# Activations at one place per quarter in 16-byte steps, low weights of the second ring 16 bytes further at each use, and a changed order of the rings

## The chip, the cores and the metric

The kernel runs on one core of a Trainium2 chip. Its time is the device time in microseconds; the median of three runs before the change is 2704.8 us (2704.26 to 2705.38). The core has five engines with queues of their own: TensorE (PE in the profile, its weight loads PEld), VectorE (DVE), ScalarE (ACT), GpSimd (POOL) and SyncE (SP), which issues most of the loads. All of them work on one on-chip memory of 128 partitions; "address" below means the byte within a partition.

## The reference

One inference step of a two-layer decoder on 256 prompt positions and 8 x 8 sample positions, 2048 features. Layer 0 mixes tokens with gated linear attention, layer 1 with a causal spatial gate; each is followed by an MLP with a squared ReLU, and each sublayer by a layer norm over the scaled residual.

```python
def sq_relu_mlp(x, w1, w2):
    return jnp.square(jax.nn.relu(x @ w1)) @ w2
...
            if i % N_MIXERS == 0:
                h, s = gla_mixer(x, gla_w_in[j], gla_w_gate[j], gla_b_gate[j], gla_norm_g[j],
                                 gla_w_out[j], gla_state0[j])
...
            else:
                h, v_rows = sg_mixer(x, sg_w_in[j], sg_b_in[j], sg_v_norm_g[j], sg_v_norm_b[j],
                                     sg_w_spatial[j], sg_b_spatial[j], sg_w_out[j])
...
            x = layer_norm(DEEPNORM_ALPHA * x + h, ln1_g[i], ln1_b[i])
            x = layer_norm(DEEPNORM_ALPHA * x + sq_relu_mlp(x, mlp_w1[i], mlp_w2[i]), ln2_g[i], ln2_b[i])
```

The arithmetic is float32; the kernel keeps it by splitting every factor into a high and a low part and adding three products.

## The kernel before

**Layout and tiles.** Prompt and sample positions stand side by side as 320 columns (`T`); the 2048 features are 16 feature tiles (`KT`) of 128 partitions. A large product `out = W^T x` is cut into column blocks of 256 output features (`UN`), which are two tiles of 128 in PSUM, and into four quarters of the input features (`NU`), four feature tiles each (`UK`). One column block of one quarter is a *unit*: a weight block of 4 x 256 columns, 512 KB in HBM.

**A unit** (`unit`, L129) loads the block into `raw` (SP's queue, three buffers), copies it to the high part `wh` on ACT (L144) and subtracts to get the low part `wl` on DVE (L145). `group` (L165) runs over the quarters and over the column blocks given, and issues for each unit 2 x 4 times the three matmuls of `mm3` (L158): low weights by high activations (L161), high weights by low activations (L162), high weights by high activations (L163). So a unit is 24 matmuls. While a matmul runs, the weights of the next one are loaded into the array.

**Rings.** `wh` and `wl` have buffers in two rings, "a" and, from layer 0's output product on, "b"; each has four buffers of each part. `next_ring` (L154) takes the rings in turn, a b a b, so quarter q of a group of one column block always finds the same ring.

**Activations.** Pairs of buffers hold a high and a low part for all 16 feature tiles: pair "a" (`a0`, `a1`) and pair "b" (`b0`, `b1`). `yh`, `yl` are the normed inputs of an MLP or of the spatial gate, `hh`, `hl` the MLP's hidden activations for 2048 of its 8192 hidden features at a time; `xh`, `xl`, `oh`, `ol` belong to layer 0's mixer; `dgh`, `dgl` are the centred activations times the norm's gain, which the first two column blocks after a norm read while the norm's own values are still being made (322 columns, the last two carry corrections).

**Where things stand.** The kernel places buffers by hand with small filler tiles. `bigtile` (L198) starts the 320 columns of a feature tile 128 bytes into the buffer (`LINE // 2` numbers of 4 bytes), and each further feature tile 1280 bytes on, which is 5 x 256. With the fillers, every activation of `x`, `o`, `y` and `h` begins at 128 past a multiple of 256, every `wh` at 0 and every `wl` at 64 (`Ring.part` puts a gap of 64 bytes before the first `wl`). `dg` starts at 0 and its feature tiles lie 1288 bytes apart, so each begins 8 bytes further than the one before. The weights of the small gate projection (`wgp`, L316 and L317) begin at 224.

**Order.** The order of instructions is made by the tile framework's scheduler from the order in which the code issues them; within an engine they then run in that order. In an MLP (`mlp`, L843) the four quarters c of the hidden features follow each other: `w1` by `y` (eight column blocks), then `w2` by `h` (eight column blocks), added into `z`. In the spatial gate `y` is read for v (L933), for u (L990) and, overwritten by the gated product, for the output (L993).

Of the kernel before, what the change touches and what calls it, by code (L numbers as in the profile page):

```python
# [9 lines left out]
F32R = mybir.dt.float32r  # L10
# [5 lines left out]
P = 128  # L16
D = 2048
KT = D // P
TP = 256
DB, DS = 8, 8  # L20
T = TP + DB * DS
# [9 lines left out]
UK = 4  # L31
UN = 256
NU = KT // UK
WARM = 9
LINE = 64
BIG = KT * T + LINE


V_BG, V_NG = 0, 8
V_L1G, V_L1B, V_L2G, V_L2B = 24, 56, 88, 120  # L40
V_SB, V_SG, V_SBB = 152, 184, 200
# [3 lines left out]
class Ring:  # L45


    def __init__(self, pool, tag):
        self.pool, self.tag, self.gap = pool, tag, False

    def part(self, p, name):

        t = self.pool.tile([P, UK, UN], F32R, tag=p + self.tag, name=name)
        if not self.gap:
            self.pool.tile([P, LINE // 4], F32, tag="gap", name=name + "_gap", bufs=1)
            self.gap = True
        return t


class Side:  # L60
# [17 lines left out]
def step_kernel(ctx: ExitStack, tc: tile.TileContext, A):  # L78
# [3 lines left out]
    def nm(s):  # L82
        uid[0] += 1
        return f"{s}_{uid[0]}"
# [11 lines left out]
    rings = [Ring(wa, "a")]  # L96
# [4 lines left out]
    def mmtile(n=T):  # L101

        if mx is not None:
            banks[0] = (banks[0] + 1) % 6
        return (mx if banks[0] > 3 else mm).tile([P, n], F32, tag="mm", name=nm("mm"), padded_shape=[P, 512])
# [19 lines left out]
    def col(c):  # L125
        return vec[:, c : c + 1]


    def unit(w, row0, q, col0, ring):  # L129

        raw = wraw.tile([P, UK, UN], F32, tag="raw", name=nm("raw"))
        src = w[row0 // (UK * P) + q, col0 // UN]
        hi = ring.part("h", nm("wh"))
        lo = ring.part("l", nm("wl"))
        units[0] += 1
        step = 2 if units[0] <= 2 else UK
        for k in range(0, UK, step):
            nc.sync.dma_start(raw[:, k : k + step, :], src[:, k : k + step, :])
        step = 1 if units[0] == 1 else step
        for k in range(0, UK, step):  # L140
            ks = slice(k, k + step)
            if units[0] == 1:
                before_unit(k)
            nc.scalar.copy(hi[:, ks, :], raw[:, ks, :])  # L144
            nc.vector.tensor_sub(lo[:, ks, :], raw[:, ks, :], hi[:, ks, :].bitcast(F32))  # L145
        return hi, lo
# [7 lines left out]
    def next_ring():  # L154
        turn[0] += 1
        return rings[turn[0] % len(rings)]
# [7 lines left out]

    def group(w, row0, cols, rh, rl, evict, side=None, width=T, before=None):  # L165

        ps = [mmtile(width) for _ in range(2 * len(cols))]
        for q in range(NU):
            if before is not None:
                before(q)  # L170
            for i, c in enumerate(cols):
                wh, wl = unit(w, row0, q, c, next_ring())
                for n in range(2):
                    for kk in range(UK):
                        k = q * UK + kk
                        mm3(ps[2 * i + n][:], wh, wl, kk, n, rh, rl, k, 0, width, k == 0, k == KT - 1)
                if side is not None:
                    side()
        for n in range(2 * len(cols)):
            evict(n, ps[n])  # L180
# [14 lines left out]
    w_in = A["gla_w_in"]  # L195
    C_Q, C_K, C_V, C_R = 0, H * DK, 2 * H * DK, 2 * H * DK + H * DV

    def bigtile(tag, dt, name, width=T):  # L198

        t = (lp if tag == "b1" else big).tile([P, BIG], dt, tag=tag, name=nm(name))
        start = LINE // 2 if width == T else 0
        return t[:, start : start + KT * width].rearrange("p (k t) -> p k t", t=width)

    def parts(pair, name, width=T):
        return bigtile(pair + "0", F32R, name + "h", width), bigtile(pair + "1", F32R, name + "l", width)

    xh, xl = parts("a", "x")  # L210
    o_all = bigtile("b0", F32, "o_all")

# [26 lines left out]
    def before_unit(k):  # L239

        x_parts(slice(k, k + 1), first_x[k // 2][:, k % 2 : k % 2 + 1, 0:T])
# [89 lines left out]
    class Head:  # L331


        def __init__(hd, h):
            hd.h = h
            hd.eb, hd.ei, hd.ee = {}, {}, {}
# [331 lines left out]
    def second_half():  # L668

        nonlocal lp, l2, z, gl, mx  # L670
        side.flush()
        split_o(range(4 * (H - 1), 4 * H))
        gst.close()
        gls.close()
        gl = ctx.enter_context(tc.tile_pool(name="gs", bufs=2, space=bass.MemoryType.PSUM))
        mx = ctx.enter_context(tc.tile_pool(name="mx", bufs=2, space=bass.MemoryType.PSUM))
        banks[0] = 3
        lp = ctx.enter_context(tc.tile_pool(name="lp", bufs=1))
        l2 = ctx.enter_context(tc.tile_pool(name="l2", bufs=2))
        wb = ctx.enter_context(tc.tile_pool(name="wb", bufs=4))  # L680
        rings.append(Ring(wb, "b"))
        wb.tile([P, LINE // 4], F32, tag="fill", name="fill_b", bufs=1)
        z = lp.tile([P, KT, T], F32, tag="z", name="z")
        lp.tile([P, 3 * LINE // 4], F32, tag="fill", name="fill_l")
        for q in range(2):
            nc.gpsimd.dma_start(z[:, 8 * q : 8 * q + 8, :], xT[:, 8 * q : 8 * q + 8, :])
# [120 lines left out]
                  lambda n, ps, i=i: evict(2 * i + n, ps), side, before=before if i == 0 else before_last if i == D // UN - 1 else None)  # L807
            i += n2

    def gemm_of(norm, out, w, col0, evict_raw, evict):  # L810

        yh, yl = parts(out, "y")
        norm.close()
        side = Side([lambda j=j: norm.apply(j, yh, yl) for j in range(KT)], 3 * NU)
        group(w, 0, (col0, col0 + UN), *norm.raw, evict_raw, side, width=TW)
        side.flush()
        for i in range(2, D // UN):
            group(w, 0, (col0 + i * UN,), yh, yl, lambda n, ps, i=i: evict(2 * i + n, ps))
        return yh, yl
# [23 lines left out]
    def mlp(i, norm, y_in, h_in, vg, vb, raw, last=False):  # L843

        w1, w2 = A["mlp_w1"][i], A["mlp_w2"][i]
        NC_ = 4
        for c in range(NC_):
            hs = []

            def sq_relu(j, x, r):  # L850
                if not hs:
                    hs.extend(parts(h_in, "h"))
                hh, hl = hs
                f = l2.tile([P, T], F32, tag="f", name=nm("f"))
                nc.vector.scalar_tensor_tensor(f[:], x, 0.0, r[:], op0=ALU.max, op1=ALU.mult)
                nc.scalar.copy(hh[:, j, 0:T], f[:])  # L856
                nc.vector.tensor_sub(hl[:, j, 0:T], f[:], hh[:, j, 0:T].bitcast(F32))  # L857

            def evict(j, ps):
                r = l2.tile([P, T], F32, tag="r", name=nm("r"))  # L860
                nc.scalar.activation(r[:], ps[:], AF.Relu)
                sq_relu(j, ps[:], r)

            def evict_raw(j, ps):
                t, wb_ = norm.correct(ps)
                r = l2.tile([P, T], F32, tag="r", name=nm("r"))
                nc.scalar.activation(r[:], t[:], AF.Relu, bias=wb_)
                sq_relu(j, r[:], r)

            if c == 0:  # L870
                yh, yl = gemm_of(norm, y_in, w1, 0, evict_raw, evict)
            else:
                gemm(w1, 0, c * D, yh, yl, evict)
            if c < NC_ - 1:
                def evz(j, ps, s=ALPHA if c == 0 else 1.0):
                    nc.vector.scalar_tensor_tensor(z[:, j, :], z[:, j, :], s, ps[:], op0=ALU.mult, op1=ALU.add)
                gemm(w2, c * D, 0, *hs, evz)
            else:
                return residual_gemm(w2, *hs, c * D, 1.0, vg, vb, raw, last=last)


    def before(q):
        if q == NU - 1:
            second_half()
        else:
            split_o(range(UK * q, UK * (q + 1)))

    norm = residual_gemm(A["gla_w_out"], oh, ol, 0, ALPHA, V_L1G, V_L1B, "b", quad=True,
                         side=side, before=before)
    norm = mlp(0, norm, "a", "b", V_L2G, V_L2B, "a")  # L890


# [21 lines left out]
    def put_v(j, x, bias):  # L914
        nonlocal v, nv
        if j == 0:
            v = bigtile("a0", F32, "v")
            nv = Norm(v, V_SG, V_SBB)
        vj = v[:, j, 0:T]
        nc.scalar.activation(vj, x, AF.Gelu, bias=bias)  # L920
        if j >= KT // 2:
            nc.vector.tensor_sub(vj, vj, nv.c[:])
        nv.add(j)
        if j == 3:
            spatial()
# [4 lines left out]
        nc.vector.tensor_add(bias[:], wb_, col(V_SB + KT + j))  # L930
        put_v(j, t[:], bias[:])

    yh, yl = gemm_of(norm, "b", A["sg_w_in"], D, ev_v_raw, lambda j, ps: put_v(j, ps[:], col(V_SB + KT + j)))  # L933

    nv.close()
    oV = A["o_vT"].rearrange("(k p) t -> p k t", p=P)
# [55 lines left out]

    norm = residual_gemm(A["sg_w_out"], ph, pl, 0, ALPHA, V_L1G + KT, V_L1B + KT, "a", quad=True)  # L993
    norm = mlp(1, norm, "b", "a", V_L2G + KT, V_L2B + KT, "b", last=True)


# [4 lines left out]
    ps = {}  # L1001
# [23 lines left out]
    for j in range(KT):  # L1025
        y, g, b = z[:, j, :], col(norm.vg + j), col(norm.vb + j)
# [4 lines left out]
        else:  # L1031
            if j not in ps:
                put_d(j)
            t = l2.tile([P, T], F32, tag="t", name=nm("t"), bufs=3)
# [70 lines left out]
```

## Time and profile before

| | before |
|---|---|
| median of 3 runs | 2704.8 us |
| the profiled execution | 2703.75 us |
| its span, first to last instruction | 2702.0 us |
| granted TensorE clock over the span | 0.999 |
| read from HBM, written | 409.60 MB, 22.02 MB |
| matmuls with `yh`, `yl` | 7872 |
| matmuls with `hh`, `hl` | 6144 |
| matmuls with `xh`, `xl`, `oh`, `ol`, of the three lines | 3072 |
| matmuls with `dgh`, `dgl`, of the three lines | 576 |

How to read the lines quoted below: a group of instructions is "line engine operation out<-in shapes xcount | busy us, mean ns of one | idle us of the engine just before them". A row of the timeline is "start us, duration us, engine line operation". A row of windows is "stretch: its length, busy time of the engine (count) clock, DMA share, GB/s". Matmuls overlap their neighbours, so the duration of one is about twice the distance between two starts.

### The profile page before, as it was taken

How to read it: one execution, taken by the hardware profiler on the slowest of the kernel's cores; microseconds unless marked ns; L12 is line 12 of the kernel's file. 1: busy time of each engine (PE TensorE's matmuls, PEld its weight loads, DVE VectorE, ACT ScalarE, POOL GpSimd, SP SyncE). 2: the span in 40 equal slices, each digit the busy share in tenths (PEclk: the TensorE clock that was granted, in tenths of full speed). 3: DMA queues.
4: the chain of work that ended last, by engine and by line, in shares of the span. 5: the costliest groups of instructions: out<-in, count | busy, mean ns of one | idle time of the engine just before them, and what ended most of it. 6: DMA issues, size and time to landing. Idle time of an engine off the chain costs nothing.

```text
span 2702.0 us, 44679 instructions
## 1 busy us (share of the span) xinstructions
PE 2692.4 (100%) x18515; PEld 2669.7 (99%) x18515; DVE 1543.5 (57%) x2289; ACT 1182.8 (44%) x1702; POOL 53.5 (2%) x83
## 2 busy tenths in 40 slices
PE   9999999999999999999999999999999999999998
PEld 9999999999999999999999999999999999999998
DVE  6667577885444444444468775587444444444456
ACT  6545455464234334333445554355334323333434
POOL 1000001000000000000001000000000000000000
PEclk9999999999999999999999999999999999999999
DMA  7656556644445455444445444454444545554442
GB/s 243 193 188 228 185 190 218 211 146 156 152 151 154 151 154 151 153 151 153 150 148 171 150 140 136 140 162 155 150 155 150 154 151 153 152 153 152 153 152 79
DMA packets 126396, 434.53 MB, mean 161 GB/s; under 512 B 13680, under 2 KB 17904, under 8 KB 126192
## 3 DMA queue, kind: packets, MB, share of 16 engines
q1 hardware_dynamic: 119136, 407.82, 48.6%
q0 software_dynamic: 6512, 23.20, 2.6%
q8 instruction: 145, 2.38, 0.4%
q10 hardware_dynamic: 544, 0.66, 0.1%
q14 instruction: 59, 0.48, 0.1%
HBM read 409.60 MB, written 22.02 MB: 160 GB/s over the span
## 4 chain that ended last, share of the span: by engine, by line
PE 99%; ACT 0%; DMA 0%; DVE 0%; issue 0%; ACTq 0%; DVEq 0%
PE mm L161 32%; PE mm L163 31%; PE mm L162 31%; PE gl L600 1%; PE gl L603 1%; PE gl L558 1%; PE gl L948 0%; PE gl L542 0%; DMA raw<-gla_w_in 0%; ACT z L1038 0%; PE gl L943 0%; DMA xr<-xT 0%; PE gl L543 0%; PE gl L458 0%; PE gl L456 0%; PE gl L521 0%
## 5 line engine op out<-in xcount | busy, mean ns | idle before, releaser
L145 DVE TENSOR_TENSOR wl<-raw,wh 128x1024 fp32r<-128x1024 f32 (+1 forms) x740 | 901.6, 1219 | 938.8 <-ACT wh L144 936.3
L144 ACT CAST wh<-raw 128x1024 fp32r<-128x1024 f32 (+1 forms) x740 | 771.3, 1044 | 1201.3 <-PE mm L163 1080.9
L163 PE MATMUL mm<-yh,wh 128*128 128x320 f32 x2624 | 805.0, 307 | 0.0
L161 PE MATMUL mm<-yh,wl 128*128 128x320 f32 x2624 | 803.1, 308 | 0.0
L162 PE MATMUL mm<-yl,wh 128*128 128x320 f32 x2624 | 794.2, 303 | 0.0
L161 PE MATMUL mm<-hh,wl 128*128 128x320 f32 x2048 | 630.8, 308 | 0.0
L163 PE MATMUL mm<-hh,wh 128*128 128x320 f32 x2048 | 628.7, 307 | 0.0
L162 PE MATMUL mm<-hl,wh 128*128 128x320 f32 x2048 | 619.6, 303 | 0.0
L162 PEld LDWEIGHTS mm<-yl,wh 128*128 128x128 f32 x2624 | 492.5, 188 | 0.0
L161 PEld LDWEIGHTS mm<-yh,wl 128*128 128x128 f32 x2624 | 490.9, 188 | 0.0
L163 PEld LDWEIGHTS mm<-yh,wh 128*128 128x128 f32 x2624 | 490.8, 187 | 0.0
L162 PEld LDWEIGHTS mm<-hl,wh 128*128 128x128 f32 x2048 | 384.4, 188 | 0.0
L161 PEld LDWEIGHTS mm<-hh,wl 128*128 128x128 f32 x2048 | 384.4, 188 | 0.0
L163 PEld LDWEIGHTS mm<-hh,wh 128*128 128x128 f32 x2048 | 383.0, 187 | 0.0
L161 PE MATMUL mm<-xh,wl 128*128 128x320 f32 x768 | 241.1, 314 | 0.9 <-DVE wl L145 0.5
L163 PE MATMUL mm<-xh,wh 128*128 128x320 f32 x768 | 236.7, 308 | 0.0
L162 PE MATMUL mm<-xl,wh 128*128 128x320 f32 x768 | 234.7, 306 | 0.0
L161 PEld LDWEIGHTS mm<-xh,wl 128*128 128x128 f32 x768 | 144.1, 188 | 5.4 <-issue 1.9
L162 PEld LDWEIGHTS mm<-xl,wh 128*128 128x128 f32 x768 | 144.3, 188 | 3.5 <-issue 1.2
L163 PEld LDWEIGHTS mm<-xh,wh 128*128 128x128 f32 x768 | 143.9, 187 | 1.3
L857 DVE TENSOR_TENSOR hl<-f,hh 128x320 fp32r<-128x320 f32 x128 | 62.3, 489 | 29.4 <-ACT hh L856 29.4
L161 PE MATMUL mm<-oh,wl 128*128 128x320 f32 x256 | 78.1, 309 | 0.6 <-DVE nw L187 0.6
(268 smaller groups left out, 2112.2 us busy)
## 6 DMA issues: line engine op xcount, KB each, us to landing
raw<-mlp_w SPq DMA_DIRECT2D x512, 512.0 KB, 3.5
raw<-gla_w_in SPq DMA_DIRECT2D x94, 512.0 KB, 4.2
raw<-sg_w_in SPq DMA_DIRECT2D x64, 512.0 KB, 3.5
st<-state SPq DMA_DIRECT2D x32, 512.0 KB, 4.3
o_state_s<-st POOLq DMA_DIRECT2D x32, 512.0 KB, 3.8
raw<-gla_w_out SPq DMA_DIRECT2D x32, 512.0 KB, 4.2
raw<-sg_w_out SPq DMA_DIRECT2D x32, 512.0 KB, 3.5
z<-xT POOLq DMA_DIRECT2D x2, 1280.0 KB, 11.6
```

The source lines that it names most:

```text
L144: nc.scalar.copy(hi[:, ks, :], raw[:, ks, :])
L145: nc.vector.tensor_sub(lo[:, ks, :], raw[:, ks, :], hi[:, ks, :].bitcast(F32))
L161: nc.tensor.matmul(ps, wl[:, kk, s], x_h, start=first, stop=False)
L162: nc.tensor.matmul(ps, wh[:, kk, s], x_l, start=False, stop=False)
L163: nc.tensor.matmul(ps, wh[:, kk, s], x_h, start=False, stop=last)
L558: nc.tensor.matmul(pu[:], hd.ktp[:, blk, kt * P : (kt + 1) * P], hd.vtp[:, blk, :], start=(blk == 0), stop=(blk == 1))
L600: nc.tensor.matmul(po[:], qm[:, kt, b * P : (b + 1) * P], part[:], start=False, stop=(b == DB - 1 and kt == 1 and part is sth))
L603: nc.tensor.matmul(pu[:], kz[:, g, i, kt * P : (kt + 1) * P], hd.vts[:, g, :], start=True, stop=True)
L857: nc.vector.tensor_sub(hl[:, j, 0:T], f[:], hh[:, j, 0:T].bitcast(F32))
```

## The change

Three things are changed for the products whose activations are `y` or `h`.

1. *Place of the activations.* A buffer of `y` or `h` is wrapped in `Rows`, which starts the four feature tiles of quarter q at `16 * places[q]` bytes past a multiple of 256 instead of 128. The MLP of layer 0 has `y` at 0, 4, 8, 12 (in 16-byte steps, quarters 0 to 3), that of layer 1 at 2, 6, 10, 14; `h` has 1, 5, 9, 13 for even c and 3, 7, 11, 15 for odd c. High and low part have the same places, but for the spatial gate, where they have 0, 2, 6, 9 and 4, 6, 8, 12.
2. *Place of the low weights in ring "b".* Its `wl` buffers are 256 bytes longer, and each use for a `Rows` product starts 16 bytes (spatial gate: 32) further than the use before in the same quarter, from 0 to 240 and round again. Each buffer of `y` or `h` has its own count, with `c0` as its start. For other products they stay at 64. Ring "a" and all `wh` keep their places.
3. *Order of the rings.* `group` takes one turn of `next_ring` more at its start for a `Rows` product, so that the units of one column block (a pair of feature tiles of the output) use the rings as a b a b and those of the next as b a b a.

```diff
+EVEN = ((0, 4, 8, 12), (2, 6, 10, 14))
+ODD = ((1, 5, 9, 13), (3, 7, 11, 15))
...
-    def __init__(self, pool, tag):
-        self.pool, self.tag, self.gap = pool, tag, False
-
-    def part(self, p, name):
-
+    def __init__(self, pool, tag, loose=False):
+        self.pool, self.tag, self.gap, self.loose = pool, tag, loose, loose
+
+    def part(self, p, name, at=None):
+
+        if p == "l" and self.loose:
+            t = self.pool.tile([P, UK * UN + LINE], F32R, tag=p + self.tag, name=name)
+            return t[:, at : at + UK * UN].rearrange("p (k n) -> p k n", n=UN)
         t = self.pool.tile([P, UK, UN], F32R, tag=p + self.tag, name=name)
...
+class Rows:
...
+    def __init__(self, buf, places, c0, cs):
+        self.buf, self.places, self.cs = buf, places, cs
+        self.c = [c0] * NU
+
+    def __getitem__(self, key):
+        p, k, t = key
+        at = 4 * self.places[k // UK] + k * T
+        return self.buf[p, at + t.start : at + t.stop]
+
+    def low(self, q):
+        c = self.c[q]
+        self.c[q] += self.cs
+        return 4 * (c % 16)
...
-    def unit(w, row0, q, col0, ring):
+    def unit(w, row0, q, col0, ring, at=LINE // 4):
...
-        lo = ring.part("l", nm("wl"))
+        lo = ring.part("l", nm("wl"), at)
...
+        if isinstance(rh, Rows):
+            next_ring()
         ps = [mmtile(width) for _ in range(2 * len(cols))]
...
-                wh, wl = unit(w, row0, q, c, next_ring())
+                ring = next_ring()
+                wh, wl = unit(w, row0, q, c, ring, rh.low(q) if ring.loose and isinstance(rh, Rows) else LINE // 4)
...
-    def bigtile(tag, dt, name, width=T):
+    def bigtile(tag, dt, name, width=T, places=None, c0=0, cs=1):
...
+        if places is not None:
+            return Rows(t, places, c0, cs)
...
-        rings.append(Ring(wb, "b"))
+        rings.append(Ring(wb, "b", True))
...
-                    hs.extend(parts(h_in, "h"))
+                    hs.extend(parts(h_in, "h", places=(ODD[c % 2], ODD[c % 2]), c0=4 * (2 * i + c // 2)))
...
-                yh, yl = gemm_of(norm, y_in, w1, 0, evict_raw, evict)
+                yh, yl = gemm_of(norm, y_in, w1, 0, evict_raw, evict, (EVEN[i], EVEN[i]))
...
-    yh, yl = gemm_of(norm, "b", A["sg_w_in"], D, ev_v_raw, lambda j, ps: put_v(j, ps[:], col(V_SB + KT + j)))
+    yh, yl = gemm_of(norm, "b", A["sg_w_in"], D, ev_v_raw, lambda j, ps: put_v(j, ps[:], col(V_SB + KT + j)),
+                     ((0, 2, 6, 9), (4, 6, 8, 12)), 2)
```

Every engine issues the same instructions as before; addresses are no part of the rows below. The scheduler moves a few rows at the start of the three stages that follow a `dg` stage. On DVE, at the end of the first `w1` product of layer 0's MLP, the casts of weights (`wl<-raw,wh`) stand among the last steps of the norm (`yl`) and the first of the hidden activations (`hl`); line numbers are 28 to 34 higher in the changed file. Before:

```order
L784 TENSOR_TENSOR t_6429<-nd_6037,z 128x320
L857 TENSOR_TENSOR hl_6373<-f_6396,hh_6372 128x320
L145 TENSOR_TENSOR wl_6797<-raw_6795,wh_6796 128x1024
L790 TENSOR_TENSOR yl_6035<-z,yh_6034 128x320
L785 SCALAR_TENSOR_TENSOR t_6423<-t_6423,vec,rstd_6038 128x320
L857 TENSOR_TENSOR hl_6373<-f_6407,hh_6372 128x320
L785 SCALAR_TENSOR_TENSOR t_6429<-t_6429,vec,rstd_6038 128x320
L145 TENSOR_TENSOR wl_6901<-raw_6899,wh_6900 128x1024
```

After:

```order
L818 TENSOR_TENSOR t_6428<-nd_6036,z 128x320
L891 TENSOR_TENSOR hl_6372<-f_6395,hh_6371 128x320
L824 TENSOR_TENSOR yl_6034<-z,yh_6033 128x320
L819 SCALAR_TENSOR_TENSOR t_6422<-t_6422,vec,rstd_6037 128x320
L891 TENSOR_TENSOR hl_6372<-f_6406,hh_6371 128x320
L819 SCALAR_TENSOR_TENSOR t_6428<-t_6428,vec,rstd_6037 128x320
L173 TENSOR_TENSOR wl_6870<-raw_6868,wh_6869 128x1024
L173 TENSOR_TENSOR wl_6840<-raw_6838,wh_6839 128x1024
```

One subtraction of weights moves from the third row to behind the norm's and the hidden activations' steps. On TensorE the same place shows the last feature tiles of `y` being used as they come, in three column blocks in turn (`mm_6436`, `mm_6569`, `mm_6570` before; numbers one lower after). Before:

```order
L162 MATMUL mm_6436<-yl_6035,wh_6528 128x320
L163 MATMUL mm_6436<-yh_6034,wh_6528 128x320
L161 MATMUL mm_6436<-yh_6034,wl_6529 128x320
L162 MATMUL mm_6569<-yl_6035,wh_6662 128x320
L163 MATMUL mm_6569<-yh_6034,wh_6662 128x320
L161 MATMUL mm_6569<-yh_6034,wl_6663 128x320
L162 MATMUL mm_6570<-yl_6035,wh_6662 128x320
L163 MATMUL mm_6570<-yh_6034,wh_6662 128x320
L161 MATMUL mm_6570<-yh_6034,wl_6663 128x320
```

After:

```order
L190 MATMUL mm_6435<-yl_6034,wh_6527 128x320
L191 MATMUL mm_6435<-yh_6033,wh_6527 128x320
L189 MATMUL mm_6435<-yh_6033,wl_6528 128x320
L190 MATMUL mm_6568<-yl_6034,wh_6661 128x320
L191 MATMUL mm_6568<-yh_6033,wh_6661 128x320
L189 MATMUL mm_6568<-yh_6033,wl_6662 128x320
L190 MATMUL mm_6434<-yl_6034,wh_6527 128x320
L191 MATMUL mm_6434<-yh_6033,wh_6527 128x320
```

The third column tile's matmuls (`mm_6569` after) come a few rows later, behind the next feature tile's for `mm_6434`. Everywhere else on TensorE the sequence of the three lines is as before.

More of the change, by code (lines that the diff above doesn't have):

```diff
@@ L196, in step_kernel, with parts @@
     C_Q, C_K, C_V, C_R = 0, H * DK, 2 * H * DK, 2 * H * DK + H * DV
-    def bigtile(tag, dt, name, width=T):
+    def bigtile(tag, dt, name, width=T, places=None, c0=0, cs=1):
         t = (lp if tag == "b1" else big).tile([P, BIG], dt, tag=tag, name=nm(name))
+        if places is not None:
+            return Rows(t, places, c0, cs)
         start = LINE // 2 if width == T else 0
         return t[:, start : start + KT * width].rearrange("p (k t) -> p k t", t=width)
-    def parts(pair, name, width=T):
-        return bigtile(pair + "0", F32R, name + "h", width), bigtile(pair + "1", F32R, name + "l", width)
+    def parts(pair, name, width=T, places=(None, None), c0=0, cs=1):
+        return (bigtile(pair + "0", F32R, name + "h", width, places[0], c0, cs),
+                bigtile(pair + "1", F32R, name + "l", width, places[1], c0, cs))
     xh, xl = parts("a", "x")
@@ L808, in gemm, with gemm_of @@
             i += n2
-    def gemm_of(norm, out, w, col0, evict_raw, evict):
-        yh, yl = parts(out, "y")
+    def gemm_of(norm, out, w, col0, evict_raw, evict, places, cs=1):
+        yh, yl = parts(out, "y", places=places, cs=cs)
         norm.close()
```

## The prediction

> **What bounds the kernel now.** I read the page's busy times and its chain first, to see which engine sets the end.
>
> ```profile
> PE 2692.4 (100%) x18515; PEld 2669.7 (99%) x18515; DVE 1543.5 (57%) x2289; ACT 1182.8 (44%) x1702; POOL 53.5 (2%) x83
> PE 99%; ACT 0%; DMA 0%; DVE 0%; issue 0%; ACTq 0%; DVEq 0%
> ```
>
> TensorE is busy for 2692.4 of 2702.0 us, and the chain that ended last lies on it for 99%. So a matmul that takes its place for a nanosecond longer moves the end by a nanosecond, and work on ACT, DVE or the queues counts only where it makes TensorE wait. The groups of instructions say which matmuls the change can reach: those whose activations are `yh`, `yl`, `hh`, `hl`.
>
> ```profile
> L163 PE MATMUL mm<-yh,wh 128*128 128x320 f32 x2624 | 805.0, 307 | 0.0
> L161 PE MATMUL mm<-yh,wl 128*128 128x320 f32 x2624 | 803.1, 308 | 0.0
> L162 PE MATMUL mm<-yl,wh 128*128 128x320 f32 x2624 | 794.2, 303 | 0.0
> L161 PE MATMUL mm<-hh,wl 128*128 128x320 f32 x2048 | 630.8, 308 | 0.0
> L163 PE MATMUL mm<-hh,wh 128*128 128x320 f32 x2048 | 628.7, 307 | 0.0
> L162 PE MATMUL mm<-hl,wh 128*128 128x320 f32 x2048 | 619.6, 303 | 0.0
> ```
>
> That is 3 x (2624 + 2048) = 14016 of the 18515 matmuls, in 584 units of 24, and none of them waited (last column 0.0). The 303 to 308 ns are lifetimes of pipelined matmuls that overlap; what counts is the distance from one start to the next. I take it from the timeline of TensorE inside a steady stage, and from a window that holds just one MLP half (256 groups of three).
>
> ```profile
> 1300.23 0.31 PE L161 MATMUL mm<-yh,wl 128*128 128x320 f32 x1
> 1300.38 0.30 PE L162 MATMUL mm<-yl,wh 128*128 128x320 f32 x1
> 1300.52 0.31 PE L163 MATMUL mm<-yh,wh 128*128 128x320 f32 x1
> 1300.66 0.31 PE L161 MATMUL mm<-yh,wl 128*128 128x320 f32 x1
> ```
>
> ```profile
> 667.13:778.06 110.93, 110.93 (x770) 1.00 0.49 152
> L161 PE MATMUL mm<-hh,wl 128*128 128x320 f32 x256 | 78.8, 308 | 0.0
> L163 PE MATMUL mm<-hh,wh 128*128 128x320 f32 x256 | 78.6, 307 | 0.0
> L162 PE MATMUL mm<-hl,wh 128*128 128x320 f32 x256 | 77.4, 303 | 0.0
> ```
>
> 110.93 us over 768 matmuls is 144.44 ns each, at a granted clock of 1.00. All of these read activations that begin 128 bytes past a multiple of 256, high weights at 0 and low weights at 64 past one. This is one fixed arrangement (worked out from the tiles' sizes and fills), kept through nearly the whole kernel.
>
> **What another arrangement costs.** The trace of before holds two other arrangements. The first is the pair of column blocks that reads the uncorrected activations `dg`: their rows have 322 columns, so each feature tile begins 8 bytes further than the one before.
>
> ```profile
> 1443.81:1472.77 28.96, 28.96 (x198) 1.00 0.48 146
> L161 PE MATMUL mm<-dgh,wl 128*128 128x322 f32 x64 | 19.9, 310 | 0.0
> L163 PE MATMUL mm<-dgh,wh 128*128 128x322 f32 x64 | 19.9, 310 | 0.0
> L162 PE MATMUL mm<-dgl,wh 128*128 128x322 f32 x64 | 19.8, 309 | 0.0
> L722 PE MATMUL gl<-lo,ones_r 128*128 128x320 f32 x2 | 0.6, 310 | 0.0
> L723 PE MATMUL gl<-hi,ones_r 128*128 128x320 f32 x2 | 0.6, 308 | 0.0
> ```
>
> 28.96 us over 196 matmuls is 147.76 ns each. Two more columns cost at most 2 x 144.44/320 = 0.9 ns of that, so some **2.4 ns** remain for the arrangement. Inside that stage the slots are uneven, as the timeline shows for its third feature tile, against 0.43 us for the three in the steady stage:
>
> ```profile
> 1444.69 0.31 PE L161 MATMUL mm<-dgh,wl 128*128 128x322 f32 x1
> 1444.83 0.31 PE L162 MATMUL mm<-dgl,wh 128*128 128x322 f32 x1
> 1444.98 0.31 PE L163 MATMUL mm<-dgh,wh 128*128 128x322 f32 x1
> 1445.14 0.31 PE L161 MATMUL mm<-dgh,wl 128*128 128x322 f32 x1
> ```
>
> Here three take 0.45 us, 150 ns each: less 0.9 for the columns that is 4.7 ns over the steady slot, the dearest end I can read. The second arrangement is the gate projection: activations at 128 as elsewhere, weights 224 bytes past a multiple of 256.
>
> ```profile
> L317 PE MATMUL gl<-xh,wgp 128*128 128x320 f32 x16 | 4.7, 308 | 0.0
> L316 PE MATMUL gl<-xl,wgp 128*128 128x320 f32 x16 | 4.7, 309 | 0.0
> ```
>
> Its mean of 308.5 ns stands 2.5 ns over the (308 + 303 + 307)/3 = 306 of the steady groups. A third reading is what it takes to come back to the steady slots. When the kernel goes from `dg` to `yh`, the first unit of 24 runs from the first of these rows to the second:
>
> ```profile
> 1472.77 0.31 PE L161 MATMUL mm<-yh,wl 128*128 128x320 f32 x1
> ...
> 1476.26 0.31 PE L161 MATMUL mm<-yh,wl 128*128 128x320 f32 x1
> ```
>
> 3.49 us against 24 x 0.14444 = 3.467: 0.023 us more, 1.0 ns per matmul, after a switch of arrangement alone.
>
> **The change part by part.** *Activations and low weights.* No matmul, copy or DMA is added or removed; 14016 matmuls get another address for their activations, and half of the L161 ones (those of the second ring) another one for their weights as well. Each unit of 24 now has a place of its own, so the arrangement switches at every unit. If the slots come back to 144.44 ns within each unit, that is 584 x 0.023 = 13 us. If they sit where `dg` and the gate projection have them, it is 14016 x 2.4 = 34 us. The bounds beyond these are nothing (place plays no part) and 14016 x 4.7 = 66 us (all as dear as the worst triple); below nothing lies a gain if some places have shorter slots than 144.44, treated as a rival. I take 1.7 ns, the middle between 1.0 and 2.4: half of the `dg` tiles start in the middle of a 16-byte step, which none does after the change, and each new arrangement is held for 24 matmuls instead of three; on the other side the sweep also visits the low weights' other 15 positions. That gives 14016 x 1.7 = **23.8 us**.
>
> *Weights' order.* An extra turn of the rings at each group makes units go a b a b, b a b a. With four buffers of each ring, the buffer of a unit was last used eight units earlier in both orders, so no load or cast is held back longer. What covers the casts:
>
> ```profile
> L145 DVE TENSOR_TENSOR wl<-raw,wh 128x1024 fp32r<-128x1024 f32 (+1 forms) x740 | 901.6, 1219 | 938.8 <-ACT wh L144 936.3
> ACT wh L144 <- PE mm L163: 1080.9, 487, 3.1
> raw<-mlp_w SPq DMA_DIRECT2D x512, 512.0 KB, 3.5
> ```
>
> ACT's casts wait 1080.9 us in 487 places for TensorE to give a buffer back, so weights are ready long ahead. A subtraction takes 1.22 us and a load lands in 3.5 us, of which the other buffers' units, at 3.47 us of matmuls each, hide several. Cost taken: 0. Without that cover a late unit would cost a load and its two casts, some 5.8 us. The few rows of DVE and TensorE that change places (shown with the change) are neighbours at the start of a stage, and cost nothing here for the same reason. The subtraction writes to an address 16 to 240 bytes further; DVE is 57% busy, so even a tenth more (90 us over the run) would hide beside TensorE.
>
> *Sum.* The profiled execution took 2703.75 us (span 2702.0 and 1.75 around it): 2703.75 + 23.8 = 2727.6. The median of the runs is 1.05 us above that execution, so I forecast **2729 us** for the median, +0.9%.
>
> **The rivals.**
> *A, the place plays no part once a unit has settled (chance 0.20).* For it: the groups of `yh` and `hh` show the same 308, 303 and 307 ns, though they lie in different buffers. Against it: these share one remainder of 256, and `dg` differs. With all units paying for the switch it is 2704.8 + 13 = 2718, with half of them 2712, with none 2705. The Trainium skill, page "SBUF — State Buffer", section "A bandwidth-pool intuition that's wrong (but worth ruling out)", gives the weight load a read port of its own beside the moving operand's, by which addresses would not matter and the time would stay at 2705. The trace doesn't agree: 146.9 ns against 144.44 at the same clock.
>
> *B, every unit runs at the level of `dg` or above (0.25).* For it: two unrelated arrangements both show 2.4 to 2.5. It gives 2704.8 + 34 = 2739, up to 2771 with the worst triple everywhere.
>
> *C, faster (0.07).* In the steady timeline the slot after L162 is 0.14 us where that after L161 is 0.15. If a place exists that makes all three slots short, about 140 ns, and most places were such, 14016 x 4.4 = 62 us would go: 2643. It decides as soon as the mean slot falls below 144.44. Against it: no triple of `dg`, over sixteen positions of the activations, undercuts the 0.43 us. The Trainium skill, page "TensorE: Matmul & The Clock Gate", section "Back-to-back issue gap", has N/2.4 + 2.5 ns for a warm matmul, 135.8 for 320 columns, which would make it 121 us less, 2584; no row here shows such a slot.
>
> *D, weights arrive late after the new ring order (0.03).* One wait of 5.8 us at each of, say, ten stages would be 58 us, 2763; the waits above speak against it. That the change does not move anything falls under A: the first ring's weights and all high weights do stay, and only their activations move.
>
> **How the numbers follow.** The forecast's own case, slots from 145.4 to 146.6 ns (2718 to 2735), has 0.45. A has 0.20, of which 0.09 lies within 0.2% (5.4 us, about what a measurement of this kernel can tell from no change) and the rest above. B has 0.25, C 0.07, D 0.03. Slower is 0.45 + 0.25 + 0.03 + 0.11 = 0.84, same 0.09, faster 0.07. The range goes from 2706, just above the place that plays no part, to 2752, which is a mean of 3.4 ns, between `dg` at 2.4 and its worst triple at 4.7; about 0.1 lies below it and 0.08 above.
>
> **What would show it.** In the profile after, windows over the MLP halves should grow from 110.93 us to between 111.7 and 112.8, while the stages of `xh` and `oh` and the two `dg` stages keep their times. The mean of L162 should rise most, from 303 towards 305 to 308, since its successor has the shortest slot now. Idle time before these matmuls should stay 0.0: any there would be D. Slots that differ by quarter of the feature tiles would show that the place decides, and in units of the second ring that the low weights' position does. Halves that stay at 110.93 would prove A, shorter ones C.

## The result and the profile after

| | before | after |
|---|---|---|
| median | 2704.73 us (2704.26 to 2705.38, 4 runs) | 2739.3 us (2739.14 to 2739.82, 4 runs) |
| profiled span | 2702.0 us | 2737.7 us |
| granted TensorE clock | 0.999 | 0.999 |

The ratio is 1.0128, with a 95% interval of 1.011 to 1.0146: slower by 34.6 us. The forecast was 2729 us in a range of 2706 to 2752; direction and range held, but the time is that of rival B, not of the forecast's own case (2718 to 2735).

The page of the kernel after shows the other engines with about the same busy time, and TensorE alone with clearly more.

```profile
PE 2727.8 (100%) x18515; PEld 2704.9 (99%) x18515; DVE 1545.1 (56%) x2289; ACT 1183.0 (43%) x1702; POOL 53.6 (2%) x83
PE 99%; ACT 0%; DMA 0%; DVE 0%; issue 0%; ACTq 0%; DVEq 0%
```

TensorE has 2727.8 - 2692.4 = 35.4 us more for as many matmuls. The groups of the three lines (L189, L190, L191 are the L161, L162, L163 of before) have these means:

```profile
L190 PE MATMUL mm<-yl,wh 128*128 128x320 f32 x2624 | 810.0, 309 | 0.0
L191 PE MATMUL mm<-yh,wh 128*128 128x320 f32 x2624 | 809.8, 309 | 0.0
L189 PE MATMUL mm<-yh,wl 128*128 128x320 f32 x2624 | 806.5, 310 | 0.0
L189 PE MATMUL mm<-hh,wl 128*128 128x320 f32 x2048 | 634.5, 310 | 0.0
L190 PE MATMUL mm<-hl,wh 128*128 128x320 f32 x2048 | 633.9, 310 | 0.0
L191 PE MATMUL mm<-hh,wh 128*128 128x320 f32 x2048 | 633.7, 309 | 0.0
```

None waited (0.0), so no weights came late. The mean of L162 goes from 303 to 309 and 310, while the others go from 308 and 307 to 310 and 309: the short slot after it is gone (by the starts, 140 ns before and 147 in the mean after). Windows over the stages of `x`, of the first `h` product and of the second `dg` pair say where the time lies. Before, the first of them was this, and the other two 110.93 and 28.96 us:

```profile
5.45:440.86 435.41, 434.93 (x2894) 1.00 0.64 208
```

After:

```profile
5.46:441.35 435.89, 435.09 (x2895) 1.00 0.63 208
668.50:782.06 113.56, 113.56 (x770) 1.00 0.47 149
1458.57:1487.52 28.95, 28.95 (x199) 1.00 0.47 146
```

The `h` product grew by 2.63 us, 3.4 ns for each of its 768 matmuls. The `dg` pair, whose addresses the change leaves alone, has its old time, and the `x` stage is 0.5 us longer. From the starts of the undisturbed units of 24 in this trace (over 530 of the 584, with no foreign matmul among their rows), the mean slot of the changed matmuls is 147.04 ns against 144.44: 2.6 x 14016 = 36 us, which accounts for all of the 35.4.

Within one product the slots differ by unit. Two units with the activations at step 5 show it in the timeline of the kernel after. Of each pair of rows the first is the unit's first matmul, the second that of the next unit; the first unit has its low weights at step 0, the second at step 9.

```profile
672.04 0.31 PE L189 MATMUL mm<-hh,wl 128*128 128x320 f32 x1
...
675.71 0.31 PE L189 MATMUL mm<-hh,wl 128*128 128x320 f32 x1
...
1974.10 0.30 PE L189 MATMUL mm<-hh,wl 128*128 128x320 f32 x1
...
1977.56 0.30 PE L189 MATMUL mm<-hh,wl 128*128 128x320 f32 x1
```

The one takes 3.67 us for its 24 matmuls, the other 3.46. These two are the longest and the shortest unit of the trace.

### The profile page after: what moved, and what is told of

The parts are those of the page before. It is cut to its first block, busy times and chain, and to the rows that moved or that the text cites. A ratio compares the mean times of both kernels' runs of the same rounds, so it can differ in the third digit from the quotient of the medians.

```text
span 2737.7 us, 44677 instructions
## 1 busy us (share of the span) xinstructions
PE 2727.8 (100%) x18515; PEld 2704.9 (99%) x18515; DVE 1545.1 (56%) x2289; ACT 1183.0 (43%) x1702; POOL 53.6 (2%) x83
## 4 chain that ended last, share of the span: by engine, by line
PE 99%; ACT 0%; DMA 0%; DVE 0%; issue 0%; ACTq 0%; DVEq 0%
PE mm L189 32%; PE mm L191 31%; PE mm L190 31%; PE gl L634 1%; PE gl L637 1%; PE gl L592 1%; PE gl L983 0%; PE gl L576 0%; DMA raw<-gla_w_in 0%; ACT z L1073 0%; PE gl L978 0%; DMA xr<-xT 0%; PE gl L577 0%; PE gl L492 0%; PE gl L490 0%; PE gl L555 0%
## 5 line engine op out<-in xcount | busy, mean ns | idle before, releaser
L190 PE MATMUL mm<-yl,wh 128*128 128x320 f32 x2624 | 810.0, 309 | 0.0
L191 PE MATMUL mm<-yh,wh 128*128 128x320 f32 x2624 | 809.8, 309 | 0.0
L189 PE MATMUL mm<-yh,wl 128*128 128x320 f32 x2624 | 806.5, 310 | 0.0
L189 PE MATMUL mm<-hh,wl 128*128 128x320 f32 x2048 | 634.5, 310 | 0.0
L190 PE MATMUL mm<-hl,wh 128*128 128x320 f32 x2048 | 633.9, 310 | 0.0
L191 PE MATMUL mm<-hh,wh 128*128 128x320 f32 x2048 | 633.7, 309 | 0.0
L190 PEld LDWEIGHTS mm<-yl,wh 128*128 128x128 f32 x2624 | 493.5, 188 | 0.0
L191 PEld LDWEIGHTS mm<-yh,wh 128*128 128x128 f32 x2624 | 493.3, 188 | 0.0
L189 PEld LDWEIGHTS mm<-yh,wl 128*128 128x128 f32 x2624 | 491.3, 188 | 0.0
L189 PEld LDWEIGHTS mm<-hh,wl 128*128 128x128 f32 x2048 | 385.7, 188 | 0.0
L191 PEld LDWEIGHTS mm<-hh,wh 128*128 128x128 f32 x2048 | 385.5, 188 | 0.0
L190 PEld LDWEIGHTS mm<-hl,wh 128*128 128x128 f32 x2048 | 385.2, 188 | 0.0
L189 PE MATMUL mm<-xh,wl 128*128 128x320 f32 x768 | 241.1, 314 | 1.5 <-DVE wl L173 0.8
L191 PE MATMUL mm<-xh,wh 128*128 128x320 f32 x768 | 236.7, 308 | 0.0
L190 PE MATMUL mm<-xl,wh 128*128 128x320 f32 x768 | 234.8, 306 | 0.0
L189 PEld LDWEIGHTS mm<-xh,wl 128*128 128x128 f32 x768 | 144.1, 188 | 6.0 <-issue 1.9
L190 PEld LDWEIGHTS mm<-xl,wh 128*128 128x128 f32 x768 | 144.3, 188 | 3.6 <-issue 1.2
L191 PEld LDWEIGHTS mm<-xh,wh 128*128 128x128 f32 x768 | 143.9, 187 | 1.3
L895 ACT ACTIVATE r<-mm 128x320 f32<-128x320 f32 x120 | 52.6, 439 | 62.5 <-PE mm L191 62.5
```

The costliest lines, as they stand in the source:

```text
L189: nc.tensor.matmul(ps, wl[:, kk, s], x_h, start=first, stop=False)
L190: nc.tensor.matmul(ps, wh[:, kk, s], x_l, start=False, stop=False)
L191: nc.tensor.matmul(ps, wh[:, kk, s], x_h, start=False, stop=last)
```

## The experiments

The theory, called P in the expectations: each pair of positions of activations and weights has a slot length of its own, and most of the positions that the sweep visits have a longer one than the arrangement of before. The rivals: the activations' places alone count (A), the sweep of the low weights alone (W), the switching from one arrangement to the next (S), or weights that come late in the new order (D). Each edit is against the changed kernel unless it says otherwise.

### One part undone at a time

**Places back to 128 for all**, low weights of ring b still moving:

```diff
-EVEN = ((0, 4, 8, 12), (2, 6, 10, 14))
-ODD = ((1, 5, 9, 13), (3, 7, 11, 15))
+EVEN = ((8, 8, 8, 8), (8, 8, 8, 8))
+ODD = ((8, 8, 8, 8), (8, 8, 8, 8))
...
-                     ((0, 2, 6, 9), (4, 6, 8, 12)), 2)
+                     ((8, 8, 8, 8), (8, 8, 8, 8)), 2)
```

> Activations of y and h all back at 128 past 256 (place 8); the low weights of ring b still move by 16 bytes, the rings still turn at each group. Theory 'each pair of positions has its own slot' (call it P): ring a units are again at the arrangement of before, 144.44 ns, or 145.2 if they need a few matmuls to come back; ring b units average 147.0, as the units of place 8 in ring b do in the profile of the changed kernel. That is 7008 x 2.5 + 7008 x (0 to 0.8) = 18 to 23 us over before: 2722 to 2728. Rival 'the places of the activations alone cost' (A): 2705. Rival 'the cost is one of switching the arrangement from unit to unit' (S): every unit still switches its low weights, so as long as the changed kernel, about 2739.

Measured: 2721.13 us, against 2704.2 before, ratio 1.0061 (1.0046 to 1.0076), 1 us under P's range. The first `h` product, which took 110.93 us before and 113.56 in the changed kernel, takes

```profile
668.46:780.29 111.83, 111.83 (x770) 1.00 0.48 151
```

From the starts in its trace, ring a's units have 144.63 ns and ring b's 146.75. A and S fall: the low weights cost 17 us by themselves; and a unit of ring a, between two units of ring b with other low weights each time, is within 0.2 ns of the steady slot. So a switch into the arrangement of before costs here about 0.2 x 24 = 5 ns a unit.

**Low weights of ring b fixed at 64**, activations at their 16 places:

```diff
-        return 4 * (c % 16)
+        return LINE // 4
```

> Activations at the 16 places as changed, low weights of ring b fixed at 64 like those of ring a, the rings still turn. P: all units are like the ring a units of the changed kernel, which average 147.1 ns: 14016 x 2.6 = 37 us over before, 2741, give or take 3. A: the same, about 2739. Rival 'the sweep of the low weights costs' (W): only the ring a half keeps a cost, and the time falls to 2722 or less. S: the place now changes by quarter only and low weights not at all, so slightly below 2739, 2730 to 2737.

Measured: 2740.3 us, ratio 1.0133 (1.0118 to 1.0149). P and A expected this, W and S did not. L162 of before has the mean that it has in the changed kernel:

```profile
L190 PE MATMUL mm<-yl,wh 128*128 128x320 f32 x2624 | 809.5, 309 | 0.0
```

The two parts, 17 us and 36 us alone, don't add up to 53 but to 34.6: once the activations stand in 16 places, it makes no difference on average whether the low weights of ring b move (ring b's units have 147.0 ns with them moving, 147.1 with them fixed).

**Both undone**, so that the order of the rings and the longer low buffers are left:

> Place 8 for all activations, low weights at 64 in both rings: what is left of the change is the order of the rings and the 256 bytes more in each low buffer of ring b. P, A, W, S: 2705, within 1 us of before. Rival 'weights come late in the new order' (D): above 2710, with idle time before L189.

Measured: 2704.41 us, ratio 1.0 (0.9991 to 1.0009). The order of the rings costs nothing, and its profile has the groups of before again:

```profile
L190 PE MATMUL mm<-yl,wh 128*128 128x320 f32 x2624 | 794.1, 303 | 0.0
ACT wh L172 <- PE mm L191: 1090.5, 490, 4.4
```

The casts wait 1090.5 us for TensorE to release buffers, as they did before the change (1080.9). D falls.

### One arrangement for all, and the same one elsewhere

**Place 13 for all**, low weights at 64 in both rings:

```diff
+EVEN = ((13, 13, 13, 13), (13, 13, 13, 13))
+ODD = ((13, 13, 13, 13), (13, 13, 13, 13))
...
+        return LINE // 4
...
+                     ((13, 13, 13, 13), (13, 13, 13, 13)), 2)
```

> One place for all activations of y and h, step 13 (208 bytes), low weights at 64 in both rings; nothing switches from unit to unit. P: every unit is like the ring a units at place 13 of the changed kernel, 150.3 ns: 14016 x 5.86 = 82 us over before, 2787. S: no switch within a product, so 2705 to 2708.

Measured: 2795.64 us, ratio 1.0337 (1.0319 to 1.0354): 91 us over before with nothing that switches. S falls for good. The groups of this kernel:

```profile
L190 PE MATMUL mm<-yl,wh 128*128 128x320 f32 x2624 | 829.4, 316 | 0.0
L191 PE MATMUL mm<-yh,wh 128*128 128x320 f32 x2624 | 818.3, 312 | 0.0
L189 PE MATMUL mm<-yh,wl 128*128 128x320 f32 x2624 | 817.2, 314 | 0.0
```

P's number was 9 us low. It took the mean of place 13's units in the changed kernel (150.3 ns), and there the first matmuls of a unit are still shorter; held throughout, it is 151.1 ns (453 for three), and 14016 x 6.7 = 93 us.

**All buffers 96 bytes further**, an edit of the kernel before (32-byte alignment makes 96 of the 80 added):

```diff
-    cp.tile([P, LINE - 8], F32, tag="fill", name="fill")
+    cp.tile([P, LINE + 12], F32, tag="fill", name="fill")
```

> The kernel before with one filler ahead of all buffers made longer, so that every buffer lies 96 bytes (six steps of 16) further: activations at step 14, low weights at 10, high weights at 6 of 16, in all stages. Theory R 'only the distances between the operands count': the same time as before, 2704 to 2706, with the same three slots of 148, 140 and 146 ns. Rival 'the remainder of an address itself counts' (an activation must begin at a multiple of 64 or 128 bytes): all 17000 large matmuls leave their arrangement, 2 to 3 ns each, 2738 to 2755.

Measured: 2704.18 us, ratio 1.0 (0.9991 to 1.001), and the means of the three lines to the nanosecond:

```profile
L163 PE MATMUL mm<-yh,wh 128*128 128x320 f32 x2624 | 805.0, 307 | 0.0
L161 PE MATMUL mm<-yh,wl 128*128 128x320 f32 x2624 | 803.1, 308 | 0.0
L162 PE MATMUL mm<-yl,wh 128*128 128x320 f32 x2624 | 794.1, 303 | 0.0
```

What counts is the distance between the operands. Activations at 224 past 256 are as good as at 128 when the weights go along: units last 3466 or 3467 ns, 144.4 a matmul. In the run with the low weights fixed, where the weights stay, the units with their activations at 224 (step 14) have 147.0 ns. The shift is a multiple of 32 bytes, so an effect of an address's remainder within 32 bytes was not tested by it; such an effect alone would not explain the slots, since in that same run steps 6 and 14 (96 and 224 bytes, both multiples of 32) cost 3.4 and 2.6 ns.

### Is the arrangement of before a floor?

Two maps, run once each, have high activations at step 8 and move other operands. In the first, ring b's units visit all pairs of positions of low and high weights once; in the second, the low activations stand apart from the high ones.

```diff
-        c = self.c[q]
-        self.c[q] += self.cs
-        return 4 * (c % 16)
+        c = Rows.uses
+        Rows.uses += 1
+        return 4 * (c % 16), 4 * (c // 16 % 16)
```

> A map: activations at step 8 throughout, ring a as before, and each unit of ring b at another pair of positions of its low and its high weights (all 256 pairs once). P: ring b units spread as in the changed kernel, 144 to 151 ns with a mean near 147, so 7008 x 2.5 = 18 us over before, 2722, give or take 4. Theory F 'the arrangement of before is at a floor': no unit below 24 x 144.4 = 3466 ns by more than 5 ns. Rival 'there are better pairs': some units at 3440 ns or less.

```diff
-                    hs.extend(parts(h_in, "h", places=(ODD[c % 2], ODD[c % 2]), c0=4 * (2 * i + c // 2)))
+                    hs.extend(parts(h_in, "h", places=((8,) * 4, ODD[c % 2]), c0=4 * (2 * i + c // 2)))
...
-                yh, yl = gemm_of(norm, y_in, w1, 0, evict_raw, evict, (EVEN[i], EVEN[i]))
+                yh, yl = gemm_of(norm, y_in, w1, 0, evict_raw, evict, ((8,) * 4, EVEN[i]))
```

> A map: high activations at step 8 throughout, low activations at the 16 places of the changed kernel, low weights of ring b moving as in it. P: what counts is each operand against the weights being loaded beside it, so units with low activations off step 8 cost as in the changed kernel for one of three matmuls at least: 1 to 3 ns in the mean, 2718 to 2745. Rival 'high and low activations must stand alike': worse than the changed kernel, above 2745. F and its rival as for the other map: no unit under 3461 ns, or some.

Measured: 2721.64 and 2731.54 us, beside 2704.23 before; both in P's ranges. The shortest undisturbed unit lasts 3464 ns in the first map and 3466 in the second, and 3464 in the changed kernel, against 3466 or 3467 for nearly every unit before. About a dozen pairs of weight positions settle at the same 433 or 434 ns for three matmuls; none settles clearly below. In these three traces nothing clearly beats the arrangement of before, so they offered no faster version to run. High and low activations need not stand alike: in the second map, units with low activations at steps 5 and 15 also last 3466 ns.

**Another arrangement from that list, in all stages**: activations at 0, low weights at 192, high at 0, an edit of the kernel before.

```diff
-            self.pool.tile([P, LINE // 4], F32, tag="gap", name=name + "_gap", bufs=1)
+            self.pool.tile([P, 3 * LINE // 4], F32, tag="gap", name=name + "_gap", bufs=1)
...
-        start = LINE // 2 if width == T else 0
+        start = 0
...
-        lp.tile([P, 3 * LINE // 4], F32, tag="fill", name="fill_l")
+        lp.tile([P, 5 * LINE // 4], F32, tag="fill", name="fill_l")
```

> Another fixed arrangement in all stages: activations at 0, low weights at 192, high weights at 0 past 256, one of those whose unit in the changed kernel settled at the length of before (433 or 434 ns for three matmuls, the unit at 3471 ns). In distances it differs from before: the high weights stand at the activations' own remainder instead of 128 away. P: 17500 large matmuls at 144.4 to 144.7 ns, so 2704 to 2710. Rival 'only the distances of before (128 and 64) have the short slots': 2.2 to 2.6 ns more for each, 2743 to 2750.

Measured: 2730.11 us, ratio 1.0095 (1.0078 to 1.0112). Neither expectation held. Most units last 3503 to 3514 ns, and a few 3466 or 3467, at the same addresses. Two windows of its profile lie one behind the other within one product and hold as many matmuls as fourteen units, 336 each; one of the first window's is a foreign one, near its end (each count includes three matmuls that reach over an edge):

```profile
1712.40:1761.50 49.10, 49.10 (x339) 1.00 0.49 151
1761.50:1810.03 48.53, 48.53 (x339) 1.00 0.50 151
```

48.53 us is fourteen units at 3467 ns. The timeline shows what lies at the start of the fast run, which lasts to the end of the product:

```profile
1758.32 0.31 PE L161 MATMUL mm<-yh,wl 128*128 128x320 f32 x1
1758.46 0.30 PE L763 MATMUL gl<-a,ones_r 128*128 128x320 f32 x1
1758.61 0.31 PE L162 MATMUL mm<-yl,wh 128*128 128x320 f32 x1
...
1759.33 0.30 PE L161 MATMUL mm<-yh,wl 128*128 128x320 f32 x1
1759.47 0.31 PE L162 MATMUL mm<-yl,wh 128*128 128x320 f32 x1
1759.62 0.31 PE L163 MATMUL mm<-yh,wh 128*128 128x320 f32 x1
1759.76 0.30 PE L161 MATMUL mm<-yh,wl 128*128 128x320 f32 x1
```

One matmul of a norm's sum (L763) fell between two of the product, and from then on three matmuls take 0.43 us, where they took 0.44 on average. So P as stated is too simple: at one set of addresses there can be more than one lasting rhythm. A unit of 24 in a map shows one of them. What decides between them is not shown: the same trace has three more L763 matmuls inside products of `y` or `h` (at 1404.48, 1522.38 and 2657.29 us), and after each of these the units go on at 3503 to 3513 ns. The arrangement of before reaches the same 3467 ns; what sets it apart in its trace is that it comes back to them, after the switch quoted in the prediction and after all four such interruptions.

**Activations in steps of 4 bytes**, 128 to 204 past 256:

```diff
+EVEN = ((32, 33, 34, 35), (36, 37, 38, 39))
+ODD = ((40, 41, 42, 43), (44, 45, 46, 47))
...
-        at = 4 * self.places[k // UK] + k * T
+        at = self.places[k // UK] + k * T
...
+                     ((48, 49, 50, 51), (48, 49, 50, 51)), 2)
```

> A map in finer steps: activations at 128 to 204 bytes past 256 in steps of 4 bytes, so that they begin at word 0, 1, 2 or 3 of a 16-byte step equally often; low weights of ring b in 16-byte steps as in the changed kernel, ring a at 64. Theory 'a row that begins inside a 16-byte step costs more, as one more step is read': the units at words 1 to 3 are longer by 0.5 ns or more a matmul than those at word 0, and the whole is 2738 to 2755. Rival 'only the distance counts, the word does not': means alike within 0.3 ns, 2733 to 2745. F: no unit settles under 433 ns for three matmuls; its rival: some do.

Measured: 2751.11 us in a single run, beside 2704.09; the time lies in the first theory's range and over the rival's. The mean slots of units at word 0, 1, 2 and 3 of a 16-byte step are 146.7, 149.8, 148.8 and 146.1 ns. So words 1 and 2 cost 3.1 and 2.1 ns more than word 0, and word 3 nothing: the word does matter, but not by the simple rule of one more step read. All weights begin at word 0 here, so the word is also a part of the distance, and this run does not tell the two apart. The shortest unit is 3465 ns.

## Why the prediction was right, and which step was off

- *TensorE's slots are the bound, and a changed slot moves the end.* Right: 35.4 us more of busy TensorE, 34.6 us more of time, idle time 0.0.
- *Another arrangement has longer slots.* Right: the new places alone cost 36 us, the new low weights alone 17, and with both undone the time is back at 2704.4.
- *2.4 ns from `dg`, 2.5 from the gate projection.* These two rows were the price: 34.6 us over 14016 matmuls is 2.5 ns. Rival B's 2739 is the time measured. That they agree so closely is in part luck. With the low weights fixed, the mean slot of one step of the activations lies anywhere from 144.9 to 150.9 ns, and nothing said that `dg` or the gate projection stood near the middle. The 2.5 was also read from lifetimes, which is not the same as slots: from 306 to 309.5 ns they rose by 3.5 in the changed kernel, where the slots rose by 2.6. By its starts the gate projection has 146.6 ns, 2.2 over the steady slot.
- *The value taken, 1.7 ns, is the step that failed, in size.* It went halfway to the 1.0 ns of a switch, on the argument that an arrangement held for 24 matmuls would come back to the steady slot. It does not as a rule: most arrangements stay at longer slots for as long as they are held (place 13 for the whole kernel: 151.1 ns). And the switch itself, priced at 23 ns a unit from one place in the trace, costs some 5 ns when the unit enters the arrangement of before. The 1.0 ns was the price of that one way in.
- *Half of the `dg` tiles start inside a 16-byte step, so `dg` is too dear a row.* Right in itself (word 2 costs 2.1 ns more than word 0 in the map, and in `dg`'s own triples 148.1 ns against 147.4), but the mean still came out at the level of `dg`.
- *L162 rises most.* Right, further than said: 309 and 310 instead of 305 to 308. The first `h` product took 113.56 us, over the 112.8 named as the upper end.
- *The order of the rings and the moved rows cost nothing.* Right: 2704.41 us with these alone.
- *Rival A, and the rule of separate ports.* Addresses do matter: moving the activations by 80 bytes with the weights left where they were cost 91 us, moving the low weights of ring b alone 17. The Trainium skill, page "SBUF — State Buffer", section "A bandwidth-pool intuition that's wrong (but worth ruling out)", gives the weight load a read port of its own. That addresses would not matter by it, which the prediction's own rows spoke against, does not hold here; whether the ports are separate, no run here tells.
- *Rival C.* No unit of any map undercut the steady slot by more than 3 ns in 3467; in the steady stream of before, the 140 ns slot exists for one matmul in three only. The prediction set beside this rival N/2.4 + 2.5 ns from the Trainium skill, page "TensorE: Matmul & The Clock Gate", section "Back-to-back issue gap". That section gives it for an isolated matmul, so it was no price for this stream, in which every matmul has a weight load of its own.

What stays open is the mechanism below the distance. With place 13 for all, successive activations stood as far from each other as before, and so did successive weights; only the activations' distance from the weights was another (and with it their remainder within 32 bytes), and it cost 91 us. That the moving operand's reads and the weight load beside it meet in the memory fits this, but no run shows where they would meet, nor why one distance gives longer slots than another. The time of the weights' own moves (17 us) may also hold a part from the distance between low and high weights.

## What to carry to other kernels

When TensorE is the bound and every matmul is alike, measure the distance between starts, not the busy time, and look for rows at other addresses in the same trace: here they priced the move better than an argument on how it might settle. Treat the distances between activations, high and low weights as a setting to be measured: a bad one held fixed cost 91 us, and when buffers must move, a shift of all of them together cost nothing (96 bytes here). Test a candidate arrangement over a whole product, with the interruptions it will meet: a short sample may show a rhythm that the kernel does not keep.

## What the runs showed of the hardware

At 320 columns and the full clock, the mean slot of a matmul went from 144.4 to 151.1 ns by address alone; one unit of the changed kernel reached 3674 ns, 153 a matmul. The shortest settled mean, 144.4 ns, came back in many arrangements, and none settled clearly lower. A stream of matmuls keeps a rhythm of several matmuls (148, 140, 146 ns in the kernel before), and at one and the same set of addresses two rhythms were seen, with means of 146.2 and 144.4 ns: the short one followed one foreign matmul and lasted to the end of the product, while three other such matmuls left the long one as it was.
